# Eight early groups in pairs for the gate and up products, and Strassen's scheme for 16 of 22 chunks of the down projection

## The chip, the cores and the metric

One NeuronCore of one Trainium2 chip runs the whole kernel. TensorE (PE) does the matrix products, ScalarE (ACT), VectorE (DVE) and GpSimd (POOL) the rest, SyncE (SP) mostly issues transfers from HBM. The metric is the device time of one execution in microseconds (us), as the median of three timed runs. One more execution was taken with a profile.

## What is computed

One layer of a decoder block in float32 with 512 positions (S), a model width of 1024 (D) and a feed-forward width of 2816 (D_FF):

```python
h = rmsnorm(x, mix_pre_g)
proj = h @ w_in                     # gMLP branch, attention branch, two gates
merged = sigmoid(g_a) * y_a + sigmoid(g_b) * y_b
x = x + rmsnorm(merged @ w_out, mix_post_g)
h = rmsnorm(x, ffn_pre_g)
x = x + rmsnorm((silu(h @ w_gate) * (h @ w_up)) @ w_down, ffn_post_g)
```

The change touches what follows `merged @ w_out`: the norm, the gate and up products and the down projection.

## The kernel before

**Exact products.** TensorE takes an operand in a reduced float32 form. So each operand is split into two parts of that form: ScalarE copies it to the high part (L70, `whi`, `ath`), VectorE subtracts that from the original and gives the low part (L71, `wlo`, `atl`), and a product is three matmuls: high x high, low x high, high x low.

```python
keep(nc.scalar.activation(out=hi, in_=src, func=AF.Copy))
keep(nc.vector.tensor_tensor(out=lo, in0=src, in1=hi.bitcast(F32), op=ALU.subtract))
```

A weight tile is 128 x 1024. It comes by a transfer of 512 KB on SP's queue into one of four `raw` buffers, and is split into one of four `whi` and one of four `wlo` buffers. `unit` and `prep_one` do so for the mixer and the down projection, `prep_job` (L725) for the gate and up products; each keeps the splits three tiles ahead of the products (AHEAD).

**The mixer** (up to 411.9 us) ends with `out_pass(1, ...)`, the last half of `merged @ w_out` for the position blocks 2 and 3. Each block of 128 positions then goes through `finish_out` (L630 to L652): a root's chain on POOL or VectorE (`rsqrt`, L164 to L174), the residual `xr`, its squares on ScalarE, a second root's chain, and `og`, the normed rows (L651, VectorE). TensorE turns `og` over (`turn`, L775: eight transposes of 128x128 a block into `ht`), and the halves and quarters of the result become the right operands `b11`, `b21`, `b22`, `t1` to `t4` (`part`, `combos`). `x2d` keeps the residual in HBM.

**Gate and up products.** The 2816 columns of w_gate and w_up are taken in 11 groups of 256. In each group the product is done by Strassen's scheme: `w_gq` holds the four quarters `a11`, `a12`, `a21`, `a22` of a group's weights; seven products, called 1 to 7, of 24 matmuls of 128x256 each (`product`, L846 to L861), take the place of eight. The left operands are `a11` (product 1), `a12` (2), `a22` (4), `a21` + `a22` (5), `a11` + `a21` (7), `s2` = `a21` + `a22` + `a11` (6) and `s2` + `a12` (3). The sums with `a22` and `a21` are made by accumulating transfers on POOL's queue (`add_to`, L692), the others by VectorE (L721, L757). Products 1 and 2 need only `b11` and `b21`, of the blocks 0 and 1. Therefore the list `jobs` begins with the products 1 and 2 of the first seven groups (NEARLY), while blocks 2 and 3 are still being normed, turned over and combined; `plan` says before which job each of these steps stands. All other products follow group by group. Behind a product 1 ScalarE copies the bank to `s` (L876); `gated` (L871) makes the 256 columns of `act` from the finished sums.

**Down projection.** 22 chunks of 128 rows of w_down; each costs 24 matmuls of 128x512 (L154 to L156), so 528. The left operand is a 128-column piece of `ath` or `atl`, the two parts of `act`. Eight banks hold the whole output. The last four chunks (RES) are done block by block, so that the end of a block (squares, L970; product with `g_fpost`, L975; root's chain; sum with the residual, L982; transfer out, L985) stands beside the next block's matmuls.

**What sets the order.** The engines run their instructions in the order that a scheduler makes of the program; only what is wrapped in `keep_in_program_order` keeps the order in which it is written. Each engine and each queue works strictly in turn, so a transfer that waits holds back those behind it on its queue. `wide` is a pool of seven tiles of 128 x 1024, shared by the rows of `finish_out` and the quarters that are added to.

Of the kernel before, what the change touches and what calls it, by code (L numbers as in the profile page):

```python
# [8 lines left out]
F32 = mybir.dt.float32  # L9
# [22 lines left out]
def trunk(ctx: ExitStack, tc: tile.TileContext, x, xt, w_n, w_f, w_u, w_ga, w_gb, w_qk,  # L32
          w_o, w_gq, w_d, pcol, b_f, w_sp, rows, out):
# [15 lines left out]
    def slot(name, dt=F32, cols=HALF):  # L49
        return stage["pool"].tile([P, cols], dt, tag="slot", bufs=stage["n"], name=name)  # L50
# [47 lines left out]
    for kc in range(NF):  # L98
        stream.append(("d", kc, w_d[kc]))
# [6 lines left out]
    RES = 4  # L106
# [16 lines left out]
    def prep_one():  # L123
# [8 lines left out]
        if kind == "d" and n >= NF - RES:  # L132
            t = stage["pool"].tile([P, 2 * D], F32R, tag="wd", bufs=RES, name=f"wd{n}")
            hi, lo = t[:, :D], t[:, D:]
        else:
            hi = st.tile([P, D], F32R, tag="whi", bufs=4, name=f"whi_{kind}{n}")
            lo = st.tile([P, D], F32R, tag="wlo", bufs=4, name=f"wlo_{kind}{n}")
# [492 lines left out]
    def finish_out(t0):  # L630
# [16 lines left out]
        for tb in reversed(two):  # L647
            r[tb] = rsqrt(e[tb - t0], ss[tb][:, 0:1], None, f"x{tb}", keep=keep)
# [76 lines left out]
    def prep_job():  # L725
# [120 lines left out]
    def product(k, b, start):  # L846
# [3 lines left out]
        if k + AHEAD >= len(jobs):  # L850
            state["end"] = len(stream)
            prep_one()
# [77 lines left out]

# [3 lines left out]
    stage["pool"], stage["n"] = dn, 14  # L934
    x2 = {}
    db = [[bank(f"d{tb}{i}") for i in range(2)] for tb in range(NT)]

    def down(kc, tb, i, w):
        o = slice(tb * P, (tb + 1) * P)
        c = slice(i * HALF, (i + 1) * HALF)  # L940
        mm3(db[tb][i], ath[kc][:, o], atl[kc][:, o], w[0][:, c], w[1][:, c], kc == 0, kc == NF - 1)

    for kc in range(NF - RES):
        halves(kc)
        w = unit("d", kc)
        halves(kc + 1)
        if kc == 2:
            g_fpost = row(3, "g_fpost")
        if 4 <= kc < 4 + NT:
            tb = kc - 4  # L950
            x2[tb] = []
            for i in range(2):
                t = slot(f"x2{tb}{i}")
                nc.sync.dma_start(out=t, in_=x2d[tb * P:(tb + 1) * P, i * HALF:(i + 1) * HALF])
                x2[tb].append(t)
        for tb in range(NT):
            for i in range(2):
                down(kc, tb, i, w)
    for kc in range(NF - RES, NF):
        halves(kc)  # L960
    last = [unit("d", kc) for kc in range(NF - RES, NF)]
    for tb in range(NT):
        end = tb == NT - 1
        ss = small(f"sd{tb}", 2)
        ts_ = [slot(f"dg{tb}{i}") for i in range(2)]
        for i in range(2):
            for kc in range(NF - RES, NF):
                down(kc, tb, i, last[kc - NF + RES])
            j = slot(f"dsq{tb}{i}")
            nc.scalar.activation(out=j, in_=db[tb][i], func=AF.Square, accum_out=ss[:, i:i + 1])  # L970
            if end and i:
                nc.scalar.activation(out=ts_[i], in_=db[tb][i], func=AF.Copy)
                nc.gpsimd.tensor_tensor(out=ts_[i], in0=ts_[i], in1=g_fpost[i], op=ALU.mult)
            else:
                nc.vector.tensor_tensor(out=ts_[i], in0=db[tb][i], in1=g_fpost[i], op=ALU.mult)  # L975
# [61 lines left out]
```

## Time and profile before

| | us |
|---|---|
| median of the timed runs (772.82 to 773.07) | 773.07 |
| profiled execution, its time | 774.62 |
| profiled execution, its span | 772.9 |
| mixer, up to the first gate product | 0 to 411.91 |
| gate and up products | 411.91 to 645.42 |
| down projection, first to last matmul | 645.42 to 764.90 |
| behind the last matmul | to 772.9 |

The page gives the busy time of each engine and its share of the span. TensorE's matmuls overlap: one is shown with 0.28 or 0.40 us, but the next begins after 0.12 or 0.23 us, so the price of one is taken from starts. The same holds for VectorE. In a timeline, what stands in brackets at a row's end is how long the engine stood idle before it and what ended that. PEclk is the clock that TensorE was granted, as a share of the full one; "DMA share" is the mean busy share of the 16 DMA engines. A name before `<-` is what is written, those behind it are what is read.

### The profile page before, as it was taken

The page shows a single profiled execution, that of the slowest core. Times are in us where ns is not written, and L with a number is a line of the kernel's source. Part 1 is how long each engine was busy: PE and PEld are TensorE (multiplying, and loading weights), DVE is VectorE, ACT ScalarE, POOL GpSimd, SP SyncE. Part 2 cuts the span into 40 slices and gives each one's busy share as a digit, 9 for nine tenths or more (in the row PEclk, how much of TensorE's full clock was granted, in tenths as well). Part 3 has the DMA queues.
Part 4 walks back from the last instruction along what each step waited for, and adds up shares of the span by engine and source line. Part 5 has one row for each costly group of instructions (what it writes and reads, how often), then busy time and mean ns, then how long its engine had stood idle before and what let it go on. Part 6 is the DMA issues. An engine that isn't in the chain of part 4 may idle for free. (4 is left out here: it accounts for less than half of the span.)

```text
span 772.9 us, 11042 instructions
## 1 busy us (share of the span) xinstructions
PE 754.0 (98%) x4294; PEld 663.3 (86%) x4294; DVE 454.7 (59%) x718; ACT 341.1 (44%) x561; POOL 137.8 (18%) x213
## 2 busy tenths in 40 slices
PE   8999999999999989999998899999999999999996
PEld 6888778888888878888888799999999998888884
DVE  4647732244325566776589599887778766334415
ACT  5343662322235544555468464444444545233312
POOL 0103000022024254444133201001010000000013
PEclk9999999999999999999999999999999999999999
DMA  8625332222232222231678769776877317332202
GB/s 293 226 72 186 114 107 93 98 82 83 84 121 96 68 96 96 74 104 56 198 291 297 199 206 262 209 191 181 206 194 184 83 58 250 129 109 87 77 0 109
DMA packets 34451, 109.55 MB, mean 142 GB/s; under 512 B 4568, under 2 KB 4824, under 8 KB 34400
## 3 DMA queue, kind: packets, MB, share of 16 engines
q1 hardware_dynamic: 30352, 94.82, 35.8%
q0 software_dynamic: 3168, 11.54, 8.6%
q10 hardware_dynamic: 880, 2.51, 0.8%
q8 instruction: 33, 0.54, 0.3%
q14 instruction: 18, 0.15, 0.1%
HBM read 104.64 MB, written 4.21 MB: 141 GB/s over the span
## 5 line engine op out<-in xcount | busy, mean ns | idle before, releaser
L154 PE MATMUL d<-whi_d,ath 128*128 128x512 f32 x144 | 56.0, 389 | 0.0
L155 PE MATMUL d<-wlo_d,ath 128*128 128x512 f32 x144 | 56.0, 389 | 0.0
L156 PE MATMUL d<-whi_d,atl 128*128 128x512 f32 x144 | 56.0, 389 | 0.0
L496 POOL TENSOR_SCALAR dm<-cb,cq 128x128 f32<-128x128 f32 (+3 forms) x32 | 40.0, 1259 | 74.4 <-DMA cb<-cdr 70.4
L692 POOL DMA_DIRECT2D a<-in_w_gq x22 | 19.2, 872 | 166.2 <-DVE s L721 49.4
L70 ACT ACTIVATE whi<-raw_a 128x1024 fp32r<-128x1024 f32 x29 | 30.6, 1058 | 28.3 <-issue 12.8
L71 DVE TENSOR_TENSOR wlo<-raw_a,whi 128x1024 fp32r<-128x1024 f32 x29 | 35.4, 1221 | 7.8 <-ACT whi L70 7.8
L71 DVE TENSOR_TENSOR atl<-act,ath 128x512 fp32r<-128x512 f32 x22 | 14.8, 691 | 42.6 <-ACT ath L70 42.6
L70 ACT ACTIVATE whi<-a 128x1024 fp32r<-128x1024 f32 x26 | 27.5, 1059 | 25.7 <-PE Y L861 10.9
L71 DVE TENSOR_TENSOR wlo<-s,whi 128x1024 fp32r<-128x1024 f32 x22 | 26.9, 1224 | 15.8 <-ACT whi L70 15.8
L70 ACT ACTIVATE ath<-act 128x512 fp32r<-128x512 f32 x22 | 13.3, 627 | 50.8 <-PE d L155 50.8
L70 ACT ACTIVATE whi<-s 128x1024 fp32r<-128x1024 f32 x22 | 23.3, 1060 | 27.5 <-PE V L861 19.2
L71 DVE TENSOR_TENSOR wlo<-a,whi 128x1024 fp32r<-128x1024 f32 x26 | 31.7, 1221 | 4.2 <-ACT whi L70 4.1
L453 POOL TENSOR_TENSOR sga<-sga,ug 128x512 f32<-128x512 f32 x8 | 14.1, 1761 | 99.7 <-ACT sga L442 99.7
L154 PEld LDWEIGHTS d<-whi_d,ath 128*128 128x128 f32 x144 | 27.0, 188 | 5.6
L155 PEld LDWEIGHTS d<-wlo_d,ath 128*128 128x128 f32 x144 | 27.0, 188 | 5.6
L156 PEld LDWEIGHTS d<-whi_d,atl 128*128 128x128 f32 x144 | 27.0, 188 | 5.5
L71 DVE TENSOR_TENSOR wlo_o<-raw_o,whi_o 128x512 fp32r<-128x512 f32 x32 | 21.1, 685 | 13.2 <-ACT whi_o L70 13.1
L861 PE MATMUL X<-b21h,whi 128*128 128x256 f32 x88 | 25.5, 290 | 2.8 <-ACT s L876 2.7
L71 DVE TENSOR_TENSOR wlo_d<-raw_d,whi_d 128x1024 fp32r<-128x1024 f32 x18 | 22.1, 1225 | 10.4 <-ACT whi_d L70 10.4
L71 DVE TENSOR_TENSOR wlo_ga<-raw_ga,whi_ga 128x1024 fp32r<-128x1024 f32 x8 | 9.8, 1225 | 29.9 <-ACT whi_ga L70 16.9
L70 ACT ACTIVATE whi_o<-raw_o 128x512 fp32r<-128x512 f32 x32 | 18.9, 624 | 18.4 <-PE o L156 7.7
(316 smaller groups left out, 2590.7 us busy)
## 6 DMA issues: line engine op xcount, KB each, us to landing
raw_a<-in_w_gq SPq DMA_DIRECT2D x36, 512.0 KB, 4.8
a<-in_w_gq SPq DMA_DIRECT2D x22, 512.0 KB, 6.5
a<-in_w_gq POOLq DMA_DIRECT2D x22, 512.0 KB, 6.8
raw_d<-in_w_d SPq DMA_DIRECT2D x22, 512.0 KB, 3.4
raw_o<-in_w_o SPq DMA_DIRECT2D x16, 512.0 KB, 3.2
raw_va<-in_w_n SPq DMA_DIRECT2D x8, 512.0 KB, 6.0
raw_u<-in_w_u SPq DMA_DIRECT2D x8, 512.0 KB, 3.3
raw_ga<-in_w_ga SPq DMA_DIRECT2D x8, 512.0 KB, 3.2
```

The source lines that it names most:

```text
L70: keep(nc.scalar.activation(out=hi, in_=src, func=AF.Copy))
L71: keep(nc.vector.tensor_tensor(out=lo, in0=src, in1=hi.bitcast(F32), op=ALU.subtract))
L154: nc.tensor.matmul(ps_ap, lh, rh, start=first, stop=False)
L155: nc.tensor.matmul(ps_ap, lh, rl, start=False, stop=False)
L156: nc.tensor.matmul(ps_ap, ll, rh, start=False, stop=last)
L453: nc.gpsimd.tensor_tensor(out=sg, in0=sg, in1=ug[j], op=ALU.mult)
L496: nc.gpsimd.tensor_scalar(out=dm[:, :n], in0=cb[:, :n], scalar1=cq[:, i, h:h + 1], scalar2=None, op0=ALU.subtract)
L692: tc.keep_in_program_order(nc.gpsimd.dma_start(out=t, in_=quad_of(g, n_), accum_op=ALU.add))
L861: nc.tensor.matmul(o, l_[:, w_], r_[:, kc, :], start=start and pair + kc + m == 0, stop=pair == 1 and kc == 3 and m == 2, skip_group_check ...
```

## The change

It has three parts. **The start of the products.** NEARLY becomes 8 and the early jobs go in pairs of groups: product 1 of two groups, then product 2 of both. The transposes of `turn` keep their place in the program. The steps for blocks 2 and 3 stand before jobs 6 to 13, not 4 to 11. Each `prep_job` loads the tiles of the next three jobs. The order of the groups becomes 0, 1, 2, 8, 3, 4, 9, 5, 6, 10, 7.

**The down projection.** Chunks 0 to 15 form four quads of four chunks; each quad is a 2x2 block matrix times `act` of two halves of chunks and of positions, and is done by Strassen's scheme with seven products of 12 matmuls of 128x512. `w_dq` is the w_down rows in that arrangement. The products of one kind stand together for all four quads, in the order 1, 2, 4, 6, 7, 5, then the six chunks left over as before ("s"), then 3. The combinations of `act` are made by VectorE in columns of 256 (`add`, `t2d`), those of the weights as for the gate products: accumulating transfers of POOL for `a21` + `a22` and `a11` + `a21`, VectorE for `s2`. `th` and `tl` are the parts of the combined `act`. Banks that a later sum needs are copied away by ScalarE (`kept`) and added later (`combine`).

**The end.** `finish` makes the norm of blocks 0 and 1 while the products 3 run, then those of 2 and 3. The last product with `g_fpost` is on VectorE straight from the bank, ahead of the root's chain, where ScalarE and POOL made it; the last transfer out is one of 512 columns, where two of 256 stood.

```diff
-    NEARLY = 7
-    order = [0, 1, 2, 7, 3, 4, 8, 5, 6, 9, 10]
-    jobs = [(g, p) for g in range(NEARLY) for p in "12"]
+    NEARLY = 8
+    order = [0, 1, 2, 8, 3, 4, 9, 5, 6, 10, 7]
+    jobs = [(g, p) for g0 in range(0, NEARLY, 2) for p in "12" for g in range(g0, min(g0 + 2, NEARLY))]
...
-        if p == "1" and g < NEARLY:
-            load(g, "a11", False)
-            load(g, "a12", False)
-        if p == "2" and g + 1 < NEARLY:
-            load(g + 1, "a11", False)
-            load(g + 1, "a12", False)
+        for g_, p_ in jobs[k:min(k + 3, 2 * NEARLY)]:
+            load(g_, "a1" + p_, False)
...
-            nc.tensor.transpose(out=b[:, k * P:(k + 1) * P], in_=x2n[tb][l][:, k * P:(k + 1) * P],
-                                identity=ident)
+            tc.keep_in_program_order(nc.tensor.transpose(
+                out=b[:, k * P:(k + 1) * P], in_=x2n[tb][l][:, k * P:(k + 1) * P], identity=ident))
...
         if k + AHEAD >= len(jobs):
-            state["end"] = len(stream)
-            prep_one()
+            prep_unit()
...
-    plan = {4: (2, "t"), 5: (3, "t"), 6: (2, 0), 7: (3, 0), 8: (2, 1), 9: (3, 1), 10: (2, 2), 11: (3, 2)}
+    plan = {6: (2, "t"), 7: (3, "t"), 8: (2, 0), 9: (3, 0), 10: (2, 1), 11: (3, 1), 12: (2, 2), 13: (3, 2)}
...
+    order_d = [(p, q) for p in "124675" for q in range(DQ)]
+    rest = list(range(4 * DQ, NF))
+    order_d += [("s", kc) for kc in rest] + [("3", q) for q in range(DQ)]
...
+    def load_sums(q):
+        if q < DQ:
+            for n_ in ("a11", "a21"):
+                dtile[q, n_] = dn.tile([P, D], F32, tag="dq", bufs=3 * DQ, name=f"{n_}d{q}")
+                nc.sync.dma_start(out=dtile[q, n_], in_=dquad(q, n_))
+            nc.gpsimd.dma_start(out=dtile[q, "a21"], in_=dquad(q, "a22"), accum_op=ALU.add)
+
+    def prep_unit():
...
+        for k_ in range(k, k + 4):
+            load_d(k_)
+        if p == "4":
+            load_sums(q + 2)
...
+            if p == "6":
+                dtile[q, "s2"] = dn.tile([P, D], F32, tag="dq", bufs=3 * DQ, name=f"s2d{q}")
+                add(dtile[q, "s2"], dtile[q, "a21"], dtile[q, "a11"])
+                nc.gpsimd.dma_start(out=dtile[q, "a11"], in_=dquad(q, "a21"), accum_op=ALU.add)
...
+            th, tl = (pair_tile(n_, 4, f"{n_}{p}{q}") for n_ in ("th", "tl"))
+            for r in range(2):
+                o = slice(r * 2 * P, (r + 1) * 2 * P)
...
+                elif p == "7":
+                    add(b12, b12, b22, ALU.subtract)
+                elif p == "4":
+                    nc.vector.scalar_tensor_tensor(out=t2s[q][:, o], in0=b11, scalar=-1.0, in1=b22,
+                                                   op0=ALU.mult, op1=ALU.subtract)
+                    add(b21, b21, t2s[q][:, o])
+                split(th[:, o], tl[:, o], t)
+                if p == "2":
+                    add(b11, b11, b12, ALU.subtract)
+        hi = st.tile([P, D], F32R, tag="whi", bufs=4, name=f"whi_d{p}{q}")
+        lo = st.tile([P, D], F32R, tag="wlo", bufs=4, name=f"wlo_d{p}{q}")
+        split(hi, lo, src)
...
+    def d_part(k, i, q=None):
+
+        p, q = order_d[k]
+        wh, wl, th, tl = dready[k]
+        b = acc[p][i]
+        for r in range(2):
+            t_ = slice(r * 2 * P + i * P, r * 2 * P + (i + 1) * P)
+            w_ = slice(r * HALF, (r + 1) * HALF)
+            for m, (l_, r_) in enumerate(((th, wh), (th, wl), (tl, wh))):
+                nc.tensor.matmul(b, l_[:, t_], r_[:, w_], start=p in "1247" and q + r + m == 0,
...
+    def finish(tb, parts, end, halves=(0, 1)):
...
+            nc.scalar.activation(out=j, in_=src(), func=AF.Square, accum_out=ss[:, i:i + 1])
+            nc.vector.tensor_tensor(out=dg[:, c], in0=src(), in1=g_fpost[:, c], op=ALU.mult)
         e = nc.vector if end else nc.gpsimd
         r = rsqrt(e, ss[:, 0:1], ss[:, 1:2], f"d{tb}")
...
+    combine("s", X, ALU.add)
+    combine("v", Z, ALU.add)
+    for i in range(2):
+        add(held["v5"][i], Y[i], held["v5"][i], ALU.subtract)
+    for i in range(2):
+        finish(i, (lambda: held["s"][i], lambda: held["v"][i]), False)
+    for i in range(2):
+        for k in range(first4, len(order_d)):
+            d_part(k, i)
+        finish(2 + i, (lambda: held["v5"][i], lambda: V[i]), i == 1, (1, 0))
```

Three places show how the order moves. In a row's names the number behind a name is that of the buffer. The first is TensorE at the first transposes of block 2, before; `whi_2_1` is product 2 of group 1, `X2` the bank of group 2, `ht20` and `ht21` the transposed halves of block 2. The first gate product begins 96 rows ahead of the transposes:

```order
L861 MATMUL X1_3738<-b21h_3511,whi_2_1_3643 128x256
L861 MATMUL X1_3738<-b21l_3512,whi_2_1_3643 128x256
L861 MATMUL X1_3738<-b21h_3511,wlo_2_1_3644 128x256
L775 MATMUL ht20_3805<-ident_112,og2_3567 128x128 x4
L775 MATMUL ht21_3812<-ident_112,og2_3567 128x128 x4
L861 MATMUL X2_3819<-b11h_3500,whi_1_2_3706 128x256
L861 MATMUL X2_3819<-b11l_3501,whi_1_2_3706 128x256
L861 MATMUL X2_3819<-b11h_3500,wlo_1_2_3707 128x256
```

The same place now, 144 rows behind the first gate product:

```order
L850 MATMUL X3_3840<-b11h_3500,whi_1_3_3741 128x256
L850 MATMUL X3_3840<-b11l_3501,whi_1_3_3741 128x256
L850 MATMUL X3_3840<-b11h_3500,wlo_1_3_3742 128x256
L765 MATMUL ht20_3873<-ident_112,og2_3569 128x128 x4
L765 MATMUL ht21_3880<-ident_112,og2_3569 128x128 x4
L850 MATMUL X2_3807<-b21h_3511,whi_2_2_3775 128x256
L850 MATMUL X2_3807<-b21l_3512,whi_2_2_3775 128x256
L850 MATMUL X2_3807<-b21h_3511,wlo_2_2_3776 128x256
```

Two more products (product 1 of the groups 2 and 3) moved ahead of the transposes, and behind them stands product 2 of group 2.

The second place is VectorE at the start of the down projection, before: behind the last sums of the gate products stand only the low parts, one `wlo_d` and one `atl` a chunk:

```order
L871 TENSOR_TENSOR act21_6291<-v610_6181,si210_6363 128x256
L71 TENSOR_TENSOR atl2_6415<-act2_3801,ath2_6414 128x512
L71 TENSOR_TENSOR atl3_6449<-act3_4525,ath3_6448 128x512
L71 TENSOR_TENSOR atl4_6487<-act4_3899,ath4_6486 128x512
L71 TENSOR_TENSOR atl5_6521<-act5_4693,ath5_6520 128x512
L71 TENSOR_TENSOR atl6_6559<-act6_3980,ath6_6558 128x512
L71 TENSOR_TENSOR atl7_6597<-act7_5104,ath7_6596 128x512
L71 TENSOR_TENSOR wlo_d4_6409<-raw_d4_6264,whi_d4_6408 128x1024
```

VectorE now, where products 4 and 6 are prepared; in `wlo_d42` the 4 is the product and the 2 the quad, `t2d` and the rows that write `act` are the sums, `s2d` those of the weights:

```order
L71 TENSOR_TENSOR tl42_6600<-act9_5339,th42_6599 128x256
L71 TENSOR_TENSOR wlo_d42_6610<-raw_d42_6506,whi_d42_6609 128x1024
L71 TENSOR_TENSOR tl42_6600<-act11_5750,th42_6599 128x256
L912 TENSOR_TENSOR act13_5918<-act13_5918,t2d3_6625 128x256
L938 SCALAR_TENSOR_TENSOR t2d3_6625<-act14_4290,act15_6294 128x256
L71 TENSOR_TENSOR wlo_d43_6637<-raw_d43_6532,whi_d43_6636 128x1024
L71 TENSOR_TENSOR tl43_6627<-act13_5918,th43_6626 128x256
L912 TENSOR_TENSOR act15_6294<-act15_6294,t2d3_6625 128x256
L912 TENSOR_TENSOR s2d0_6652<-a21d0_6384,a11d0_6382 128x1024
L71 TENSOR_TENSOR tl43_6627<-act15_6294,th43_6626 128x256
```

Between the low parts now stand sums of 256 and of 1024 columns, and a low part of `act` comes in two rows.

The third place is VectorE at the end of the program, before; `d30` is a bank of the last block, `v_d3` to `t_d3` are its root's chain:

```order
L982 SCALAR_TENSOR_TENSOR dg21_7114<-dg21_7114,y_d2_7146,x221_6602 128x512
L975 TENSOR_TENSOR dg30_7163<-d30_6376,g_fpost0_6452 128x512
L164 TENSOR_SCALAR v_d3_7196<-sd3_7162 128x1
L168 TENSOR_SCALAR y_d3_7197<-v_d3_7196 128x1
L170 TENSOR_SCALAR w_d3_7198<-v_d3_7196 128x1
```

VectorE now, at the same place; `Vd1` is the bank that the last matmul writes:

```order
L1053 SCALAR_TENSOR_TENSOR dg2_7333<-dg2_7333,y_d2_7341,x22_7167 128x512 x2
L1048 TENSOR_TENSOR dg3_7382<-v5d1_7019,g_fpost_7056 128x512
L1048 TENSOR_TENSOR dg3_7382<-Vd1_6393,g_fpost_7056 128x512
L157 TENSOR_SCALAR v_d3_7389<-sd3_7381 128x1
L161 TENSOR_SCALAR y_d3_7390<-v_d3_7389 128x1
```

Both products with `g_fpost` now stand ahead of the chain.

## Rows read from the trace of the kernel before

**Rows 1.** The page, section 1: busy us, share of the span, instructions.

```profile
PE 754.0 (98%) x4294; PEld 663.3 (86%) x4294; DVE 454.7 (59%) x718; ACT 341.1 (44%) x561; POOL 137.8 (18%) x213
```

**Rows 2.** Waits of TensorE: line waited for, us in total, times, longest.

```profile
PE ht L775 <- DVE og L651: 3.3, 1, 3.3
PE X L861 <- ACT s L876: 2.7, 3, 1.5
...
PE V L861 <- ACT whi L70: 0.8, 1, 0.8
```

**Rows 3.** Windows: us, PE, PEld, DVE, ACT, POOL busy, PEclk, DMA share, GB/s.

```profile
411.90:429.40 17.50, 12.18 (x98) 11.59 (x96) 15.78 (x33) 11.95 (x19) 10.00 (x19) 0.99 0.91 342
...
466.76:645.42 178.66, 178.66 (x1489) 178.66 (x1490) 141.53 (x166) 85.69 (x113) 14.83 (x18) 1.00 0.65 175
645.42:765.30 119.88, 119.87 (x530) 98.95 (x528) 45.59 (x54) 35.60 (x54) 7.44 (x27) 1.00 0.30 101
```

**Rows 4.** Chain of waits: start, us, what ran; mark at 466.76.

```profile
465.65 1.07 ACT whi L70
466.76 6.02 PE V L861 x48
...
475.66 5.76 PE V L861 x48
```

**Rows 5.** Timeline of TensorE, first and last down matmul: start, us, instruction.

```profile
645.42 0.40 PE L154 MATMUL d<-whi_d,ath 128*128 128x512 f32 x1
...
764.90 0.39 PE L156 MATMUL d<-wd,atl 128*128 128x512 f32 x1
```

**Rows 6.** Timeline of TensorE, first products and the transposes of both blocks.

```profile
411.91 0.28 PE L861 MATMUL X<-b11h,whi 128*128 128x256 f32 x1
...
429.40 1.94 PE L775 MATMUL ht<-ident,og 128*128 128x128 f32 x8 [3.35 <-DVE og L651]
430.99 0.56 PE L861 MATMUL X<-b11h,whi 128*128 128x256 f32 x1
...
434.56 1.03 PE L775 MATMUL ht<-ident,og 128*128 128x128 f32 x8
435.36 0.36 PE L861 MATMUL X<-b11h,whi 128*128 128x256 f32 x1
```

**Rows 7.** Timeline of VectorE, `og` and rows of 256, 512 and 1024 columns.

```profile
427.96 2.48 DVE L651 SCALAR_TENSOR_TENSOR og<-xr,y_x,g_pre 128x1024 f32<-128x1024 f32 x2 [0.69 <-POOL y_x L174]
...
440.76 0.42 DVE L871 TENSOR_TENSOR act<-X,si 128x256 f32<-128x256 f32 x1 [3.15 <-ACT si L870]
441.10 0.68 DVE L785 TENSOR_TENSOR hf<-hf,hf 128x512 f32<-128x512 f32 x1
441.70 1.22 DVE L71 TENSOR_TENSOR wlo<-raw_a,whi 128x1024 fp32r<-128x1024 f32 x1
442.84 0.69 DVE L785 TENSOR_TENSOR hf<-hf,hf 128x512 f32<-128x512 f32 x1
```

**Rows 8.** DMA: queues (packets, MB, share of 16 engines); accumulating transfers of L692.

```profile
q1 hardware_dynamic: 30352, 94.82, 35.8%
q0 software_dynamic: 3168, 11.54, 8.6%
...
a<-in_w_gq POOLq DMA_DIRECT2D x22, 512.0 KB, 6.8
...
DMA to landing us min/median/max: 5.2/6.8/9.5
```

**Rows 9.** Timeline of the end, VectorE, ScalarE and the last transfer's issue.

```profile
747.00 0.69 DVE L975 TENSOR_TENSOR dg<-d,g_fpost 128x512 f32<-128x512 f32 x1 [13.19 <-ACT dsq L970]
...
765.38 0.60 ACT L970 ACTIVATE dsq<-d 128x512 f32<-128x512 f32 x1 [2.09 <-PE d L156]
...
766.10 0.21 DVE L164 TENSOR_SCALAR v_d<-sd 128x1 f32<-128x1 f32 x1 [0.20 <-ACT dsq L970]
...
769.91 0.35 ACTq L985 DMA_DIRECT2D out_y<-dg  x1
```

More of the change, by code (lines that the diff above doesn't have):

```diff
@@ L131, in prep_one @@
         raw = raws.pop(i)
[L132 to L137, printed above, removed]
+        hi = st.tile([P, D], F32R, tag="whi", bufs=4, name=f"whi_{kind}{n}")
+        lo = st.tile([P, D], F32R, tag="wlo", bufs=4, name=f"wlo_{kind}{n}")
         small_steps = i == 0 or kind[0] in "qko"
@@ new lines, in load_d @@
+    def load_d(k):
+        if k < len(order_d) and k not in draw:
+            p, q = order_d[k]
+            src = {"1": "a11", "2": "a12", "3": "a12", "4": "a22"}
+            if p in src or p == "s":
+                draw[k] = st.tile([P, D], F32, tag="raw", bufs=NRAW, name=f"raw_d{p}{q}")
+                nc.sync.dma_start(out=draw[k], in_=w_d[q - 4 * DQ] if p == "s" else dquad(q, src[p]))
+    def load_sums(q):
[4 more added lines that the diff above has]
+            nc.gpsimd.dma_start(out=dtile[q, "a21"], in_=dquad(q, "a22"), accum_op=ALU.add)
@@ L933, in trunk @@
     dn = dnx.enter_context(tc.tile_pool(name="dn", bufs=1, reuse_waits="tile"))
[L934 to L963, printed above, removed]
+    for q in range(2):
+        load_sums(q)
+    V, X, Y, Z = ([bank(f"{n_}d{i}") for i in range(2)] for n_ in "VXYZ")
+    acc = {"1": V, "6": V, "5": V, "3": V, "2": X, "7": Y, "4": Z}
+    def d_part(k, i, q=None):
+        p, q = order_d[k]
+        wh, wl, th, tl = dready[k]
[5 more added lines that the diff above has]
+                nc.tensor.matmul(b, l_[:, t_], r_[:, w_], start=p in "1247" and q + r + m == 0,
+                                 stop=q == DQ - 1 and r == 1 and m == 2,
+                                 skip_group_check=True)
@@ new lines, in d_plain @@
+    def d_plain(k):
+        kc = order_d[k][1]
+        wh, wl, th, tl = dready[k]
+        for banks, tb0, i in ((X, 0, 0), (Z, 0, 1), (Y, 2, 1), (V, 2, 0)):
+            for j in range(2):
+                t_, w_ = slice((tb0 + j) * P, (tb0 + j + 1) * P), slice(i * HALF, (i + 1) * HALF)
+                for m, (l_, r_) in enumerate(((th, wh), (th, wl), (tl, wh))):
+                    nc.tensor.matmul(banks[j], l_[:, t_], r_[:, w_], start=False, stop=m == 2,
+                                     skip_group_check=True)
@@ L964, in trunk @@
+    def finish(tb, parts, end, halves=(0, 1)):
         ss = small(f"sd{tb}", 2)
[L965 to L968, printed above, removed]
+        dg, x2r = row_tile(f"dg{tb}"), rows_d[tb]
+        for i, src in zip(halves, parts):
+            c = slice(i * HALF, (i + 1) * HALF)
             j = slot(f"dsq{tb}{i}")
[L970 to L975, printed above, removed]
+            nc.scalar.activation(out=j, in_=src(), func=AF.Square, accum_out=ss[:, i:i + 1])
+            nc.vector.tensor_tensor(out=dg[:, c], in0=src(), in1=g_fpost[:, c], op=ALU.mult)
@@ L1010 @@
     part = lambda i: w[:, i * D:(i + 1) * D]
+    wd, DQ = a["w_down"][0].reshape(NF, P, D), 4
     arrays = {
```

107 lines of the change are left out of this document (82 added, 25 removed).

## Prediction

> **What bounds the kernel now.** I read the busy shares first: TensorE is busy 98% of the span [rows 1], so time can go only where TensorE waits or where it has fewer instructions. Its waits come next: two groups in the middle, 3.3 us for `og` of finish_out and 2.7 us for the copy `s` [rows 2]. The windows place the rest: from 466.76 to 645.42 (the gate and up products) and from 645.42 to 765.30 (the down projection) TensorE is busy to the last 0.01 us, while VectorE works 141.53 of 178.66 us in the first and 45.59 of 119.88 us in the second [rows 3]. What is left is the stretch in which those products start, 411.91 to 466.76, and the 7.6 us behind the last matmul.
>
> A 128x256 product matmul costs 0.12 us (48 in 5.76 us), a product of 24 so 2.88 us [rows 4]. A 128x512 matmul of the down projection costs 0.2267 us: the first of 528 starts at 645.42, the last at 764.90 [rows 5].
>
> **Part 1, the start of the products (eight groups ahead, in pairs).** The mark is the first matmul of product 6 of the second group, at 466.76 [rows 4]. Ahead of it stand 15 products and 16 transposes. Eight transposes take 0.80 us where nothing disturbs them (434.56 to 435.36), so TensorE alone needs 15 x 2.88 + 1.60 = 44.80 us from 411.91 [rows 6]; it took 54.85. The 10.05 us are lost to the waits of [rows 2], 0.8 us for `whi` at the mark among them (ScalarE starts it at 465.65, TensorE its matmul at 466.76) [rows 4], to transposes that take 1.59 instead of 0.80 us right behind the long wait (429.40 to 430.99) [rows 6], and for the rest to restarts and slow matmuls behind the waits.
>
> In the changed order every first product of a pair is followed by the other group's first product, so the copy `s` has 2.88 us to finish; its 2.7 us go. Six products instead of four stand ahead of the transposes of block 2, so TensorE reaches them at 411.91 + 6 x 2.88 = 429.19; in the old trace they started at 429.40, when the first `og` (427.96, half of 2.48 us) had landed [rows 6, 7]. VectorE's order up to `og` is the same but for which `wlo` stand there and one place, so I leave `og` where it is: 0.2 us of wait remain. With the wait the slow matmuls go too. What is late next is VectorE. Its starts stand 1.14 us apart for 1024 columns, 0.60 for 512 and 0.34 for 256 [rows 7]. From `og`'s end at 430.36 to the `s` sum of the second group it has 11 `wlo` and 3 sums (14 x 1.14), 18 rows of 512 (10.8) and 6 `act` (2.0): 28.8 us, to 459.2. Added to that are the waits that its order forces, an estimate from 2.88 per product and 1.07 per `whi`: 2.2 us for two ScalarE results of products just ended, 1.2 us for the `whi` of the first sum. So 462.6, and 1.07 for the last `whi` [rows 4]: the mark at 463.7. TensorE alone would be there at 411.91 + 17 x 2.88 + 1.60 + 0.2 = 462.7, so it waits 1.0 us, as today. Two more products are done by then: the gain is 466.76 + 5.76 - 463.7 = 8.8 us. Bounds: 9.8 if VectorE is never late, 3.9 if the wait for `og` and its slow matmuls stay (rival 2).
>
> Nothing else of this part is on the path. The eighth group trades two ScalarE copies for two VectorE additions (1.2 us, in a stretch where VectorE has 37 us free [rows 3]) and loads `a11` and `a12` of one more group a second time: two transfers of 512 KB. One of those costs all 16 DMA engines 35.8% x 772.9 / 94.82 MB x 0.524 MB = 1.53 us [rows 8]. SP's queue still stands behind `og` at the same transfer; the `raw` loads that are queued behind it are needed four products later, 11.5 us, when even the slowest accumulating transfer (9.5 us) would have landed [rows 8].
>
> **Part 2, the down projection.** A unit of seven products costs 12 matmuls where a chunk costs 24: 28 x 12 + 6 x 24 = 480 instead of 528, on the same tiles and columns. 48 x 0.2267 = 10.9 us [rows 5]. The order shows TensorE's rows without a break between the last gate product and the first of these. Whether they run without a wait depends on who prepares them, in 2.72 us per unit:
>
> VectorE does per unit `wlo` (1.14) and two `tl` (0.68): 1.8 us for products 1 and 5; two 256-column sums more for 2 and 7 (2.5); four more for 4 (3.2); one 1024-column sum more for 6 and 3 (3.0). That is over 2.72 for 4 and 6, by 0.5 and 0.3: eight units, 3.2 us (the products 3 are prepared beside the plain chunks, which give 5.44 us each). Ahead of them are the products 1 and 2, with 0.9 and 0.2 to spare, and the order lets VectorE run until the four `whi` buffers stop it. Walking its order from the last gate product (time 0): the last `wlo` of product 2 is done at 15 (due at 19), the last of 4 at 25 (due 30), the last of 6 at 37 (due 41). It is never later than TensorE. All its work in the stage, 31 `wlo`, 50 `tl`, 32 small and 8 wide sums, 14 of 512 columns, is 31 x 1.14 + 82 x 0.34 + 8 x 1.14 + 14 x 0.6 = 81 us of 109. Cost 0, with 2.5 us if the 256-column rows cost their full time (rival 1).
>
> First a row: a VectorE instruction of 256 columns lasts 0.42 us and the next starts after 0.34; one of 1024 lasts 1.22 and holds the engine 1.14 [rows 7]. [...]
>
> The DMA engines carry 8 `raw`, 8 tiles for sums and 8 accumulating transfers from POOL until the products 7 need the last. An accumulating one costs 8.6% x 772.9 / 11.54 x 0.524 = 3.0 us of all engines [rows 8]. Five of the plain ones are issued before time 0; 11 x 1.53 + 8 x 3.0 = 41 us remain, due by 49.5, when the last product 7 has to be split. That is thin but the stretch from 411.90 ran at a 0.91 share [rows 3]. SP's queue stops once, for the last gate matmul, ahead of the second `a21`; behind it stands `raw` of the last product 2, needed 19 us later. Cost 0, up to 26 (rival 3).
>
> **Part 3, the end.** Before, the last block's Square (765.38) was followed by the root's chain on VectorE at 766.10, while ScalarE and POOL made the last product with `g_fpost`; the last transfer was issued at 769.91 [rows 9]. Now that product stands on VectorE between the two, and waits for the Square as the one at 747.00 did [rows 9]: +0.6 us. Two sums of 512 columns take 0.1 us less than 512 + 2 x 256. The last transfer is 256 KB, not 128. Together +0.5; bounds 0 and 1.2.
>
> **Sum.** -8.8 - 10.9 + 0.5 = -19.2 us. The profiled execution (span 772.9, itself 774.62) becomes a span of 753.7; the median of the timed runs is 773.07, so 753.9.
>
> **Rivals.** (1) VectorE paces the second stage: every row costs its duration, so 4, 6 and 7 take 3.7, 3.3 and 2.9 us. Its lead after product 2 (about 5 us) is used up by 4 x 1.0 + 4 x 0.6 + 4 x 0.2, and three early `atl` of 0.69 come on top: TensorE waits some 3 us, 757. For it: VectorE is as full in the gate products' first groups; against it: the starts in [rows 7]. Chance 0.13. (2) `og` comes later than in the old trace, as TensorE and ScalarE ask for more `wlo` and `whi` ahead of it, so the transposes, now pinned, wait 3.3 us and run slow again (1.6 us): 8.8 becomes 3.9, and 758.8. Against it: the order around the root's chain hardly moves. Chance 0.10. (3) On the other side: the eight accumulating transfers run one after the other. The slowest of 22 took 9.5 us to land [rows 8]; 8 x 9.5 = 76 us, where the last is due at 49.5: TensorE waits 26.5 us, 780.4. It decides from (49.5 + 19.2) / 8 = 8.6 us each in series. Against it: 22 of them ran beside the gate products, two in a group, and TensorE waited for none; two in a row there had 14.4 us. Chance 0.04. That the change does nothing is excluded by the 480 rows in the order.
>
> **How the numbers follow.** The forecast, 752 to 756, has 0.68; rivals as above; 0.05 is for causes that I do not see, half of it below 752. The range runs from 751.5 (all of 9.8, no cost at the end) to 759.0 (rival 2). About 0.2% (1.5 us) can be told from no change; every case but rival 3 and a part of the unseen lies beyond it: faster 0.94, same 0.02, slower 0.04.
>
> **What would show it.** Right: no TensorE wait for `og` over 0.5 us, the mark at 463 to 464 on the new count, the last gate product ending near 636.5, 480 matmuls in 109 us, about 8 us behind them. Wrong: a wait for `og` or slow matmuls near 430 (rival 2), waits of TensorE for `wlo_d` or `tl` in products 6 and 7 (rival 1), or for `whi` of sums behind POOL's transfers (rival 3).

## The result and the profile after

The changed kernel takes 760.36 us (median of 4 runs, 759.25 to 762.13); the kernel before took 772.95 us beside it (4 runs, 772.79 to 773.07). The ratio is 0.9839, interval 0.982 to 0.9859: 12.6 us faster. That is the direction that was forecast, but 6.5 us short of it, and outside the range of 751.5 to 759.0. The profiled execution has a span of 757.6 us and is itself the one of 759.25 us. By stages, from the starts of the first and last matmuls:

| stage, us | before | after | change | forecast |
|---|---|---|---|---|
| mixer, to the first gate product | 411.91 | 411.40 | -0.5 | 0 |
| gate and up products | 233.51 | 224.62 | -8.9 | -8.8 |
| down projection, first to last matmul's start | 119.48 | 109.38 | -10.1 | -10.9 |
| from the last matmul's start to the end | 8.03 | 12.15 | +4.1 | +0.5 |

The page's busy times, against [rows 1]: TensorE has 48 instructions fewer, VectorE 102 more.

```profile
PE 740.1 (98%) x4246; PEld 652.2 (86%) x4246; DVE 501.3 (66%) x820; ACT 365.0 (48%) x618; POOL 148.0 (20%) x220
```

The waits of TensorE, as in [rows 2] (line waited for, us in total, times, longest). The waits for `og` and for `s` are gone; one for a `wlo_d` of the down projection is new.

```profile
PE V L850 <- ACT whi L70: 0.8, 1, 0.8
PE Vd L1005 <- DVE wlo_d L71: 0.5, 1, 0.5
```

The windows, as in [rows 3] (us; busy time of PE, PEld, DVE, ACT, POOL; PEclk, DMA share, GB/s), at the new boundaries: first product, first transposes, mark, first down matmul, 650, the wait, end of the last matmul, end.

```profile
411.40:428.60 17.20, 17.20 (x145) 17.20 (x143) 15.59 (x33) 13.65 (x21) 9.98 (x19) 1.00 0.94 341
428.60:463.12 34.52, 33.68 (x282) 33.43 (x281) 31.23 (x43) 21.95 (x36) 3.52 (x5) 1.00 0.84 240
463.12:636.02 172.90, 172.90 (x1440) 172.90 (x1441) 140.21 (x169) 82.65 (x111) 14.65 (x17) 1.00 0.67 181
636.02:650.00 13.98, 13.98 (x64) 11.58 (x63) 13.98 (x31) 11.44 (x23) 1.72 (x2) 1.00 0.97 317
650.00:675.00 25.00, 24.52 (x110) 19.96 (x108) 21.93 (x38) 13.66 (x24) 5.21 (x6) 1.00 1.05 319
675.00:745.79 70.79, 70.79 (x311) 58.31 (x311) 52.44 (x80) 35.27 (x65) 10.11 (x22) 1.00 0.36 109
745.79:757.60 11.81, 0.00 (x0) 0.00 (x0) 6.62 (x17) 0.69 (x2) 1.88 (x6) 0.70 0.34 127
```

The stretch with 5.3 us of idle TensorE in [rows 3] (17.50 us, 12.18 busy) is full now. Two new things are to be seen: from 636 to 675 the DMA engines are full (0.97, 1.05) and VectorE has no free moment up to 650; and behind the last matmul stand 11.8 us, where [rows 3] and [rows 9] left 7.6.

The transposes of block 2 in TensorE's timeline (compare [rows 6]) start without a wait, and the product behind them 0.85 us later, not 1.59:

```profile
428.54 0.28 PE L850 MATMUL X<-b11h,wlo 128*128 128x256 f32 x1
428.66 1.09 PE L765 MATMUL ht<-ident,og 128*128 128x128 f32 x8
429.51 0.36 PE L850 MATMUL X<-b21h,whi 128*128 128x256 f32 x1
```

The chain of waits in the down projection (start, us, what) shows where the 0.5 us come from: a load of `a21` issued at 652.16, the accumulating transfer behind it, VectorE's sum `s2` for product 6, its split, TensorE.

```profile
652.16 9.90 DMA a21d<-in_w_dq
...
662.62 9.94 DMA a21d<-in_w_dq
672.56 0.02 issue
672.58 0.04 DVE s2d L912
672.62 1.11 issue
673.73 1.23 DVE wlo_d L71
```

VectorE's timeline shows it idle ahead of that sum, so the transfer was late and not VectorE:

```profile
672.58 1.22 DVE L912 TENSOR_TENSOR s2d<-a21d,a11d 128x1024 f32<-128x1024 f32 x1 [1.28 <-DMA a21d<-in_w_dq]
```

And the end in the timelines of POOL and VectorE (compare [rows 9]); the last matmul starts at 745.40:

```profile
734.08 0.29 POOL L157 TENSOR_SCALAR v_d<-sd 128x1 f32<-128x1 f32 x1 [59.11 <-ACT dsq L1047]
...
734.94 1.40 POOL L166 TENSOR_SCALAR t_d<-y_d,w_d 128x1 f32<-128x1 f32 x1
...
739.13 0.29 POOL L157 TENSOR_SCALAR v_d<-sd 128x1 f32<-128x1 f32 x1
...
743.90 0.29 POOL L157 TENSOR_SCALAR v_d<-sd 128x1 f32<-128x1 f32 x1
743.96 1.42 DVE L1053 SCALAR_TENSOR_TENSOR dg<-dg,y_d,x 128x512 f32<-128x512 f32 x2 [2.15 <-POOL y_d L167]
...
748.21 1.41 DVE L1053 SCALAR_TENSOR_TENSOR dg<-dg,y_d,x 128x512 f32<-128x512 f32 x2 [1.63 <-POOL y_d L167]
749.54 0.68 DVE L1048 TENSOR_TENSOR dg<-v5d,g_fpost 128x512 f32<-128x512 f32 x1
750.14 0.68 DVE L1048 TENSOR_TENSOR dg<-Vd,g_fpost 128x512 f32<-128x512 f32 x1
750.74 0.20 DVE L157 TENSOR_SCALAR v_d<-sd 128x1 f32<-128x1 f32 x1
```

The root's chains of blocks 0, 1 and 2 run one after the other on POOL, from 734.08 to 748.2, 4.3 to 5.1 us each. VectorE's sum of block 2 waits for the third, and the last block's product, whose bank is complete at 745.8, stands behind that sum until 750.14.

### The profile page after: what moved, and what is told of

Read it like the earlier page. It is cut to its first block, busy times and chain, and to the rows that moved or that the text cites. A ratio compares the mean times of both kernels' runs of the same rounds, so it can differ in the third digit from the quotient of the medians.

```text
span 757.6 us, 11165 instructions
## 1 busy us (share of the span) xinstructions
PE 740.1 (98%) x4246; PEld 652.2 (86%) x4246; DVE 501.3 (66%) x820; ACT 365.0 (48%) x618; POOL 148.0 (20%) x220
## 4 chain that ended last, share of the span: by engine, by line
PE 85%; DVE 6%; DMA 4%; POOL 2%; issue 1%; ACT 1%; SPq 0%; DVEq 0%; POOLq 0%; ACTq 0%
PE V L850 13%; PE Y L850 8%; PE X L850 4%; DMA a21d<-in_w_dq 3%; PE Vd L1005 2%; PE vs L147 2%; PE vs L148 2%; PE o L148 2%; PE o L147 2%; PE o L149 2%; PE vs L149 2%; PE u L147 2%; PE q L148 2%; PE q L149 2%; PE ga L148 2%; PE u L149 2%
## 5 line engine op out<-in xcount | busy, mean ns | idle before, releaser
L71 DVE TENSOR_TENSOR wlo_gb<-raw_gb,whi_gb 128x1024 fp32r<-128x1024 f32 x8 | 9.8, 1225 | 28.5 <-ACT whi_gb L70 15.5
L147 PE MATMUL vs<-whi_vs,xgh 128*128 128x512 f32 x64 | 25.6, 403 | 0.9 <-ACT whi_vs L70 0.9
L71 DVE TENSOR_TENSOR wlo_k<-raw_k,whi_k 128x512 fp32r<-128x512 f32 x16 | 11.3, 715 | 22.0 <-ACT whi_k L70 22.0
L850 PE MATMUL V<-t2h,whi 128*128 128x256 f32 x88 | 25.0, 284 | 0.8 <-ACT whi L70 0.8
L147 PE MATMUL o<-whi_o,mgh 128*128 128x512 f32 x64 | 25.6, 400 | 0.0
L147 PE MATMUL ga<-hth,whi_ga 128*128 128x512 f32 x64 | 25.5, 399 | 0.0
L148 PE MATMUL vs<-wlo_vs,xgh 128*128 128x512 f32 x64 | 25.5, 398 | 0.0
L1005 PE MATMUL Vd<-wlo_d,th 128*128 128x512 f32 x64 | 25.0, 391 | 0.5 <-DVE wlo_d L71 0.5
L148 PE MATMUL o<-wlo_o,mgh 128*128 128x512 f32 x64 | 25.4, 398 | 0.0
L149 PE MATMUL o<-whi_o,mgl 128*128 128x512 f32 x64 | 25.4, 397 | 0.0
```

The source lines that it names most:

```text
L147: nc.tensor.matmul(ps_ap, lh, rh, start=first, stop=False)
L148: nc.tensor.matmul(ps_ap, lh, rl, start=False, stop=False)
L149: nc.tensor.matmul(ps_ap, ll, rh, start=False, stop=last)
L850: nc.tensor.matmul(o, l_[:, w_], r_[:, kc, :], start=start and pair + kc + m == 0, stop=pair == 1 and kc == 3 and m == 2, skip_group_check ...
L1005: nc.tensor.matmul(b, l_[:, t_], r_[:, w_], start=p in "1247" and q + r + m == 0, stop=q == DQ - 1 and r == 1 and m == 2, skip_group_check ...
```

## The experiments

**The parts alone.** First the start of the products alone, in the kernel before.

```diff
-    NEARLY = 7
+    NEARLY = 8
```

(with `order`, `jobs`, `plan`, `prep_job` and `turn` as changed.)

> The kernel before with the first part of the change alone: eight groups in pairs, transposes in program order, the steps for blocks 2 and 3 two jobs later; the old down projection. Theory A (the start of the products gave what was forecast, the miss lies behind the gate products): 773.0 - 9.0 = 764.0 us, mark 51.6 us behind the first gate product, no TensorE wait for og over 0.5 us, runs within 0.5 us of each other. Rival B (the early part is what scatters, since the DMA share is about 0.9 there): 764 to 766 with runs 1 to 3 us apart.

Measured: 765.92 us (6 runs, 764.52 to 769.06; before 774.21 in 11 runs), ratio 0.9902 (0.988 to 0.9924). The gate products are 224.65 us long, the down projection 119.48 and the end 8.35 (8.03 before). The forecast of part 1 holds. That runs lie 1 to 4 us apart is not a matter of this part: those of the kernel before went from 771.82 to 776.17 here.

Then the other half, the changed kernel with the old start.

```diff
-    NEARLY = 8
+    NEARLY = 7
```

> The changed kernel with the old start of the products (seven groups, old order, old plan): the Strassen down projection and the new end alone. By the forecast's terms -10.9 + 0.5: 762.6 us. Theory A (the end behind the last matmul is 12.2 us instead of 7.6, and the DMA engines are full from 0 to 39 us of the down projection): 773.0 - 10.9 + 4.6 + 0.5 to 2 = 767.2 to 768.7, with runs 1 to 3 us apart. Rival B: 767 with runs within 0.5 us.

Measured: 768.93 us (6 runs), ratio 0.993 (0.9909 to 0.9951). Gate products 233.56, down projection 110.07 with a wait of 0.8 us for `wlo_d`, end 12.24 us. So the two parts don't disturb each other, and of the stages that the change touches only those behind the gate products miss their forecast. The changed kernel itself, again:

> The changed kernel again, as it is, beside the three others on the same chip. Gate products 224.6 us, down projection 109.4 to 110.4, 12.2 us behind the last matmul's start; the time of the mixer varies by up to 2 us with the point at which TensorE gets its full clock in the first 10 us, so 759 to 762.

Measured: 760.0 us (4 runs, 759.34 to 761.84; before 773.05), gate products 224.61, down projection 110.27 with a wait of 1.4 us, end 12.1.

**The start: the steps for blocks 2 and 3 at their old place.**

```diff
-    plan = {6: (2, "t"), 7: (3, "t"), 8: (2, 0), 9: (3, 0), 10: (2, 1), 11: (3, 1), 12: (2, 2), 13: (3, 2)}
+    plan = {4: (2, "t"), 5: (3, "t"), 6: (2, 0), 7: (3, 0), 8: (2, 1), 9: (3, 1), 10: (2, 2), 11: (3, 2)}
```

> The changed kernel with the steps for blocks 2 and 3 two jobs earlier again (before jobs 4 to 11, the old plan): four products ahead of block 2's transposes, everything else as changed. Theory A (what removes the wait for og is that six products stand ahead of the transposes, since og itself comes where it came before): TensorE reaches the transposes 11.5 us behind the first gate product, og is there some 16 to 17 us behind it, so TensorE waits 4 to 6 us and its next matmuls are slow for 1 to 2 us; about 1 us of it comes back because VectorE was the late one at the mark: gate products 229 to 231 us long instead of 224.6. Rival F (the pairs and the copy s give the gain, not the place of the transposes): 224.6 to 226.

Measured: 767.95 us (before 774.81); the gate products are 231.84 us long, 7.2 more than in the changed kernel (229 to 231 were expected). Its longest wait of TensorE, and the windows of the wait and of what follows:

```profile
PE ht L765 <- DVE og L645: 5.7, 1, 5.7
```

```profile
409.94:427.31 17.37, 11.66 (x97) 11.49 (x96) 15.78 (x33) 12.01 (x19) 10.12 (x19) 0.93 0.92 341
427.31:432.00 4.69, 4.69 (x23) 4.69 (x24) 2.52 (x3) 1.20 (x2) 0.00 (x0) 0.53 0.86 180
```

It is the six products ahead of the transposes that take the wait away; the pairs and the eighth group without them leave 1.7 of the 8.9 us. The wait is longer than the 3.3 us of the kernel before because TensorE is there earlier: four products behind the first matmul, without the waits for `s`. No run tries the transposes' fixed place in the program order by itself.

**The transfers of the down projection.** The changed kernel without its eight accumulating transfers (those sums are left out of the computation):

```diff
-            nc.gpsimd.dma_start(out=dtile[q, "a21"], in_=dquad(q, "a22"), accum_op=ALU.add)
...
-                nc.gpsimd.dma_start(out=dtile[q, "a11"], in_=dquad(q, "a21"), accum_op=ALU.add)
```

> The changed kernel without the eight accumulating transfers of the down projection (a22 isn't added to a21, nor a21 to a11; the sums are left out of the computation). Theory A (these transfers fill the DMA engines from 636 to 675 us and make the sums of product 6 late): the 0.5 us wait of TensorE for wlo_d goes, the DMA share in that stretch falls from 1.0 to about 0.6, runs lie within 0.5 us of each other, 759.0 us. Rival D (VectorE, busy to the last 0.01 us from 636 to 650, paces that stretch): wait and scatter stay, 760.4.

Measured: 757.97 us (4 runs, 757.05 to 760.3; before 774.21). TensorE has no wait for `wlo_d`, and the down projection is 108.6 us long: 479 x 0.2267, the forecast's own term. Its windows, where those of the changed kernel are 636.02 to 675:

```profile
636.25:650.00 13.75, 13.75 (x63) 11.39 (x62) 13.75 (x31) 11.21 (x22) 0.00 (x0) 1.00 0.95 349
650.00:675.00 25.00, 25.00 (x112) 20.71 (x111) 25.00 (x43) 16.04 (x28) 0.00 (x0) 1.00 0.49 187
```

VectorE now works without a gap for 38.75 us, and TensorE doesn't wait: VectorE is full but not late, against rival 1 of the prediction and rival D of this run. The runs still scatter, so the transfers are not what scatters.

Making `a21` + `a22` with POOL's arithmetic (together with the mended end of e6, below):

```diff
-            nc.gpsimd.dma_start(out=dtile[q, "a21"], in_=dquad(q, "a22"), accum_op=ALU.add)
...
+                nc.gpsimd.tensor_tensor(out=dtile[q, "a21"], in0=dtile[q, "a21"], in1=draw[k], op=ALU.add)
```

> As e6_blocks_chain2, and a21 + a22 of the down projection made by POOL's arithmetic from the a22 tile that product 4 loads anyway, instead of by accumulating transfers. Theory A (the DMA engines are full there): four accumulating transfers of about 3 us of all engines go, the wait of TensorE for wlo_d goes and the down projection is 108.6 us long instead of 109.4 to 110.4; 4.1 to 5.5 us below the changed kernel. Rival E (POOL's sums and VectorE get in each other's way, and VectorE is full there): the down projection stays at 109.4 or grows.

Measured: 767.16 us (6 runs; before 773.05), the down projection 120.55 us long, 6.3 more than in e6. Theory A's remedy was wrong and rival E right: the line's own view (duration in ns: least, median, most) and VectorE's timeline behind it.

```profile
L923 POOL TENSOR_TENSOR a21d<-a21d,raw_d x4: 2386/2956/14229, 648.0 to 667.8; 128x1024 f32<-128x1024 f32 x4
```

```profile
659.51 0.42 DVE L911 TENSOR_TENSOR act<-act,t2d 128x256 f32<-128x256 f32 x1
662.22 3.40 DVE L911 TENSOR_TENSOR s2d<-a21d,a11d 128x1024 f32<-128x1024 f32 x1 [2.29 <-POOL a21d L923]
665.54 2.58 DVE L71 TENSOR_TENSOR tl<-act,th 128x256 fp32r<-128x256 f32 x1
```

Of POOL's four sums the shortest took 2.39 us; the longest took 14.23 while VectorE ran without a gap from 648 to 660, and ended when VectorE had stood idle for 2.29 us. Then VectorE's rows became 3 to 6 times as long (a 1024-column sum 3.40 us, where the next one took 1.21 at 670.92; a 256-column row 2.58, where the one at 659.17 took 0.42) beside POOL's next sums.

**The end.** The chains of blocks 1 and 2 on VectorE:

```diff
-        e = nc.vector if end else nc.gpsimd
+        e = nc.vector if tb else nc.gpsimd
```

> The changed kernel with the root's chains of blocks 1 and 2 on VectorE instead of POOL; block 0 stays on POOL. Theory A (three chains of 4.3 to 5.1 us in a row on POOL hold VectorE's rows of the last block, which stand behind block 2's sum): VectorE takes the last bank at 745.9 + 0.6 instead of 750.1, so the time behind the last matmul falls from 12.2 to about 8.6 us: 760.4 - 3.6 = 756.8. Rival C (the last block's own path costs it: product with g_fpost on VectorE ahead of the chain and 256 KB in the last transfer): no change, 760.4.

Measured: 758.35 us (before 774.21), end 10.9 us: 1.3 of the 3.6 us. Its VectorE waits for block 0's chain until 742.00, and has the work of three blocks behind that; it takes the last bank at 751.70, with the last matmul at 748.20. So it was not enough to move chains; blocks 0 and 1 come too late, which the next runs test. In these the last three plain chunks give blocks 0 and 1 first, and `finish` of these blocks stands ahead of the preparation of the last products 3:

```diff
+            d_plain(k, (0, 1) if q >= rest[-3] else range(4))
...
+    for k in range(first4 - 3, first4):
+        d_plain(k, (2, 3))
```

> The changed kernel in which the last three plain chunks give their matmuls for blocks 0 and 1 first (banks X and Z of three chunks, then Y and V of the three); the chains stay on POOL. All matmuls and sums are the same. Theory A, sharpened by the run before (blocks 0 and 1 come too late, so that all of VectorE's end work and three POOL chains are pressed into the last 15 us): chains 0 and 1 are done before the last products 3, chain 2 alone ends some 0.5 us behind the last matmul, VectorE takes the last bank about 1.9 us behind it and not 4.3: the time behind the last matmul's start falls from 12.2 to 9.8 us, the median by 2.4. Rival C (the last block's own path costs it): 12.2 as before.

And with block 2's chain on VectorE as well:

```diff
-        e = nc.vector if end else nc.gpsimd
+        e = nc.vector if tb >= 2 else nc.gpsimd
```

> As e5_blocks_first, and the root's chain of block 2 on VectorE. Theory A: VectorE has nothing late at the last matmul any more; it takes the last bank 0.6 us behind it: 8.5 us behind the last matmul's start, the median 3.6 us below that of the changed kernel. Rival C: 12.2.

Measured: the end is 8.54 and 8.56 us, but the down projection 114.14 and 114.21, and the medians 760.87 and 761.73 (before 773.05). The end is as short as theory A says for e6, and shorter than the 9.8 us that it says for e5; the gain is lost in front of it. In e5 the lost time itself helps: TensorE comes late, so that POOL's last chain is done when it ends. TensorE's timeline of e6:

```profile
738.56 0.39 PE L1005 MATMUL Vd<-whi_d,th 128*128 128x512 f32 x1
741.48 0.80 PE L1005 MATMUL Vd<-wlo_d,th 128*128 128x512 f32 x1 [2.53 <-DVE wlo_d L71]
742.07 0.63 PE L1005 MATMUL Vd<-whi_d,tl 128*128 128x512 f32 x1
742.50 0.63 PE L1005 MATMUL Vd<-whi_d,th 128*128 128x512 f32 x1
```

and VectorE's there:

```profile
738.88 1.41 DVE L1053 SCALAR_TENSOR_TENSOR dg<-dg,y_d,x 128x512 f32<-128x512 f32 x2 [2.25 <-POOL y_d L167]
740.21 2.35 DVE L71 TENSOR_TENSOR wlo_d<-s2d,whi_d 128x1024 fp32r<-128x1024 f32 x2
```

The `wlo_d` of the last products 3 stand on VectorE behind a sum that waits for POOL. The next two write these preparations ahead of the finish and take POOL out of VectorE's way, in e10 with all chains on VectorE, in e11 with block 0's alone on POOL:

```diff
+    while dstate["next"] < len(order_d):
+        prep_unit()
     for i in range(2):
         finish(i, (lambda: held["s"][i], lambda: held["v"][i]), False)
...
-        e = nc.vector if end else nc.gpsimd
+        e = nc.vector
```

> The changed kernel with the last three plain chunks by blocks, as in e5_blocks_first, the preparation of the last three products written ahead of the finish of blocks 0 and 1, and all root's chains on VectorE, so that nothing on VectorE waits for POOL. Theory A (in e5 and e6 the gain at the end was lost because the weights of products 3 stood on VectorE behind a sum that waited for POOL's chain; the end itself is mended): the 2.5 us wait for wlo_d near 740 and the slow matmuls behind it go; 8.5 us behind the last matmul's start, the down projection 109.4 to 110.4: 3.6 us below the changed kernel, 756 to 757. Rival G (VectorE has too much to do there in any order): waits of 1 to 3 us stay in front of the last products.

```diff
-        e = nc.vector
+        e = nc.vector if tb else nc.gpsimd
```

> As e10_ends_dve, with the chain of block 0 alone on POOL: VectorE's sum for block 0 waits for it once, at a place where the weights of products 3 have 1 to 2 us to spare. Theory A: as e10, within 0.5 us. Rival G: waits of 1 to 3 us in front of the last products.

Measured: 757.15 us and 757.09 us (before 774.81); ratios 0.9771 (0.975 to 0.9791) and 0.9784 (0.9759 to 0.9808). End 8.53 and 8.59 us, down projection 110.44 and 110.91. The wait near 740 is gone in e10; in e11 1.0 us of it is left. In e10 VectorE takes the last bank 1.1 us behind the last matmul's start (748.17), where it took it 4.7 us behind it, and waits for ScalarE's Square alone:

```profile
749.31 0.69 DVE L1048 TENSOR_TENSOR dg<-Vd,g_fpost 128x512 f32<-128x512 f32 x1 [1.25 <-ACT dsq L1047]
```

Theory A holds for the end: it falls by 3.6 us, from 12.15 to 8.5. The runs don't part the two remedies fully: the chains alone gave 1.3 us (e3), and the earlier blocks alone were run only with the wait of e5. Last, with e10, the loads of the sums earlier:

```diff
-        if p == "4":
-            load_sums(q + 2)
+        if p == "2" and q >= 2:
+            load_sums(q)
```

> As e10_ends_dve, with the loads of a11 and a21 of the quads 2 and 3 and their accumulating transfers two units (5.4 us) earlier in the program, ahead of two raw tiles of product 4 instead of behind them. Theory A (the last sum for product 6 comes late because its chain of three transfers of some 10 us each starts late, behind raw on SP's queue): the wait for wlo_d near 675 goes and the down projection is 108.6 to 109.0 us long: 0.5 to 1.5 us below e10. Rival H (the DMA engines are simply full until 675, whatever the order): a wait of 0.5 to 2 us stays, there or in product 4.

Measured: 755.77 us (4 runs, 754.61 to 757.29; before 774.81), ratio 0.9753 (0.9731 to 0.9774); down projection 109.68, the wait for `wlo_d` 0.5 us where e10 had 1.5. That is no proof of theory A: with the loads at their old place this wait was 0.5 us in the changed kernel's profile and up to 1.5 in others (e3, e8). What is left of it goes with rival H, as the DMA share from 650 to 675 is 1.05 here too. The windows of that stretch and of the end:

```profile
650.00:675.00 25.00, 24.54 (x108) 19.64 (x107) 21.32 (x39) 11.67 (x22) 4.96 (x6) 1.00 1.05 312
...
744.74:752.90 8.16, 0.00 (x0) 0.00 (x0) 3.91 (x12) 0.69 (x2) 0.00 (x0) 0.72 0.31 116
```

This kernel beats the kernel before and the changed one: its slowest run, 757.29, lies below the fastest of the changed kernel (759.25).

## Why the prediction was right in its first half and wrong in its second

**Part 1 was right, term by term.** The mark came at 463.12, 51.72 us behind the first product, where 51.79 were forecast. TensorE reached the transposes at 428.66, VectorE's first `og` was there, and no slow matmuls followed. Rival 2 did not come: the first `og` ends 17.2 us behind the first product, as in the kernel before (17.3). No run makes its case, a later `og`, so its price of 4.9 us stays open; e9 lost 7.2 in another way, with two products fewer ahead of the transposes.

**Part 2: the count was right, "cost 0" was not.** 48 matmuls fewer are worth 10.9 us when nothing waits (e4). The step that failed is the one on the DMA engines. It set the deadline by the products 7 ("due by 49.5"), but `s2` of product 6 reads `a21` after `a22` has been added to it, and is due some 10 us earlier. Ahead of that sum stand two transfers one after the other, and they took 9.90 and 9.94 us, while the walk of VectorE's order took the sums to be there and the median of [rows 8] was 6.8. The engines' full share was seen as thin and still priced at nothing. In the changed kernel's order it costs 0.5 to 1.5 us of wait, 0.8 to 1.8 in the length of the stage. Rival 3 named the transfers too, but not this: it had all eight accumulating transfers in series, and the last two of `a21` overlapped (issued at 659.79 and 662.62, landing after 8.2 to 9.9 us). What ran in series was each quad's load and the transfer that adds to it. Rival 1 fell: VectorE had no free moment for 38 us and was never late (e4).

**Part 3 failed.** The term was +0.5, measured +4.1. Its step followed the last block alone: Square, product, chain, sum, transfer. It took for granted that VectorE is free when the last bank is complete. In the kernel before a block's chain, 3.2 us on POOL, stood beside the next block's 24 matmuls, and VectorE's sum of block 2 was under way before the last matmul at 764.90:

```profile
763.88 1.41 DVE L982 SCALAR_TENSOR_TENSOR dg<-dg,y_d,x 128x512 f32<-128x512 f32 x2 [2.59 <-POOL y_d L174]
```

The change makes blocks 0 and 1 complete only with the last plain chunk, so three chains of 4.3 to 5.1 us and their sums are pressed into the last 15 us, and VectorE took its rows in turn: the last block's product, whose bank is complete at 745.8, began at 750.14, behind the sum of block 2. The order gave a hint: VectorE's sum of block 2 stands ahead of the last block's products. It stands there in the old order too; what had to be followed is when the chain that it waits for is done. e10 and e11 show it: with blocks 0 and 1 earlier and VectorE's last sums off POOL's chains, the end is 8.5 and 8.6 us, which is the forecast's 8.0 + 0.5. So the last block's own path was priced rightly, and what stood ahead of it was left out. With that mended (e10, 757.15 us) the time lies inside the range.

**The rest.** 3.6 us at the end and 0.8 in the down projection make 4.4 of the 6.5. The remaining 2 us fit the mixer, which the change doesn't touch: its length lies near one of three values, 410, 411.5 or 413 us (the last section). The four runs of before were all as short as the first value gives (409.9 + 233.5 + 119.5 + 8.0 = 770.9 us of span, and 1.7 around it: 772.6); of the changed kernel's four spans (757.6, 758.5, 758.8, 760.4) none is. That is worked out from profiled runs; the timed runs have no trace, so it isn't shown for them. Compared by stages the change is worth 14 to 15 us.

## What to carry to other kernels

An engine that takes its rows in turn, as VectorE did here (it began the last block's product 4.3 us after the bank was complete), is free at the end only if everything queued ahead of the last block is done by then: follow each earlier block's chain, on POOL too, as carefully as the last. For a sum in several steps, the deadline is that of its first reader, and transfers that depend on one another count one after the other, at the length they have while the engines are full (here 9.90 and 9.94 us at a DMA share of 1.05, where the median beside the gate products was 6.8). To fill a wait, count how many products must stand ahead of the instruction that waits, and check who is late next.

## What the runs showed of the hardware

**TensorE's clock after a wait.** Behind waits of 0.48 us (the changed kernel), 1.38 (e8) and 1.52 (e10) for `wlo_d` the first two matmuls started 0.33 to 0.34 us apart and the next ones 0.22 to 0.24; the granted clock of the changed kernel was 1.00 there (675 to 680). Behind 2.53 us (e6) the next seven matmuls of 512 columns started 0.42 to 0.59 us apart instead of 0.227, which cost 1.7 us on top of the wait; the granted clock was 0.72 from 740 to 746, and 1.00 from 746 to 753. Behind 5.7 us (e9) the granted clock was 0.53 for 4.7 us. Behind a wait of 1.97 us in the mixer both happened, as the next paragraph shows.

**Three lengths of the same mixer.** The kernel before and the changed kernel run the same TensorE instructions there. In 14 profiled runs the first gate product starts between 409.94 and 413.40: four times near 410, five near 411.5, five near 413. Two places make it, some 1.5 us each. One is the start: in the changed kernel's run the matmuls start 0.43 us apart until 9.6 us (0.23 from 9.9 on), in that of the kernel before only until 7.3; the granted clock of the profile is 1.00 there in both (5 to 12 us) and does not show it. The other lies behind a wait of TensorE for `qk`, 1.97 us in the kernel before, which ends at 278.64, and 1.96 in the changed one. Behind it matmuls of 512 columns start 0.43 us apart in the kernel before, until 282.0 (granted clock 0.53 from 278.6 to 282.0), and 0.23 us apart in the changed one (1.00). Over 276 to 288 the granted clock was 0.86 in the kernel before, e6, e8 and e10, and 1.00 in the changed kernel, e11 and e12; no run shows what decides. First the kernel before, then the changed one, with the granted clock third from the end:

```profile
276.00:288.00 12.00, 10.03 (x44) 8.48 (x42) 7.85 (x24) 5.50 (x16) 6.94 (x9) 0.86 0.21 67
```

```profile
276.00:288.00 12.00, 10.04 (x56) 8.55 (x55) 8.79 (x27) 6.86 (x19) 7.09 (x8) 1.00 0.26 86
```

Differences of under 3.5 us between single runs of this kernel mean nothing until the stages have been compared.

**POOL beside VectorE.** In e7 a 1024-column sum of POOL took 14.23 us under VectorE's rows without a gap; the shortest of the four took 2.39. At the end of the changed kernel a 1-column row of POOL's chain took 1.40 us (734.94) beside VectorE's wide rows, where 0.34 is the median of its nine. In e7 POOL's long sum ended at 662.19, only after 2.29 us without a row on VectorE, and VectorE's rows of 3.40 and 2.58 us (662.22 and 665.54) stand beside POOL's next sums. What makes them longer no run shows.
